# Hybrid decoder layer on one core: lo parts of weights by accumulating transfers, a fused softmax mask and maximum, decays built by transfers

## The chip, the cores and the metric

The kernel runs on one core of a Trainium2 chip. The core has five instruction streams that run beside each other: TensorE (PE, matrix products; its loads of the stationary operand are shown as PEld), VectorE (DVE), ScalarE (ACT), GpSimd (POOL) and SyncE (SP), which only issues transfers here. Sixteen DMA engines carry the transfers of all streams. Products are accumulated in PSUM; everything else lies in SBUF. Each stream takes its instructions strictly in order.

The metric is the device time of one execution, in microseconds (us). Three runs of the kernel before gave 473.19, 473.93 and 474.29 us; the median is 473.93.

## The reference

One decoder layer of 512 tokens and 1024 channels, in float32. The input is normalised, projected by one matrix of 1024 x 4384, and feeds three head groups. Their outputs are gated, concatenated (1536 wide), projected back, added to the input and normalised.

```
proj = rmsnorm(x) @ w_in
A: kc, vc = compress(k_c), compress(v_c)        # blocks of 32 tokens every 16, 2048 -> 256 -> 64
   o_a = g0*attend(q, kc, vc) + g1*attend(q, k_s, v_s, selected) + g2*attend(q, k_w, v_w, window)
B: a_cs = cumsum(dt * a) per chunk of 128 tokens
   decay_in = exp(where(causal, a_cs[l] - a_cs[s], -inf))
   y = ((C @ B.T) * decay_in) @ xdt + (C @ state) * exp(a_cs) + x * d_skip   # scan over 4 chunks
C: o_c = softmax(q @ km.T / sqrt(128)) @ vm,  km, vm = rmsnorm(mem) @ w_mem_kv
out = rmsnorm(x + [silu(gate)*o_a, norm(y*silu(z)), silu(gate)*o_c] @ w_out)
_masked_softmax: s = where(mask, s, -1e30); p = exp(s - max(s)) * mask; p / max(sum(p), 1e-30)
```

With 512 tokens all blocks are selected and the window reaches back to the start, so the selected and the window branch are both plain causal attention, over their own keys and values: 8 heads, 2 branches, 2 groups of keys.

## The kernel before

**Exactness by two parts.** Products run in float32r, PE's fast form of float32 with a shorter mantissa. Every operand that needs full precision is therefore split: hi is the operand rounded to float32r, lo the rest, and a product is taken as hi x hi, lo x hi and hi x lo, accumulated in one PSUM tile. Weights are split too. `chunk` (L379-390) does that for one block of at most 128 x 1024: SP loads it into `wst` (2 slots), ACT or DVE copies it into `whi`, and DVE or POOL subtracts `wst - whi` into `wlo` (3 slots each). There are 64 such blocks: 28 column tiles of the input projection (`wd`), the two halves of z (`wz0`, `wz1`), the values (`wv`), the compression (`w1k`, `w1v`), memory keys and values (`wmk`, `wmv`) and the output projection in three shares (`wob`, `wox`, `woa`). The first of all is forced onto ACT.

**What sets the order.** The program is recorded as streams, and a list scheduler (`Program.issue`, L173) puts the instructions of each engine in an order that is fixed when the kernel is built. It uses its own costs (`Program.cost`, L137), by which a transfer takes 60 ns of its issuing engine and 2000 ns plus bytes/360 until it lands, on one shared transfer resource. Of the instructions that could go it takes the first of the program, shifted by a bias; some instructions may go to either of two engines, and the one that is free takes them (`AnyEngine`, L290: a copy to ACT or DVE, a two-operand operation to DVE or POOL). On the chip every engine then follows its list, and waits where an operand is late.

**Stages.** First the input rows are normalised and turned, and the z projection starts. Then come the eight convolution tiles of group B with z's other half, then, woven together, the scan of group B (`ssd_decay`, `ssd_mix`, `ssd_out`) and the compressed keys and values, memory keys and values, rotated keys and value rows. From about 211 us on attention (`attention`, L733) is woven with the query and gate tiles, group C (`xa_scores`, `xa_apply`) and the output shares of groups B and C (`out_part`, L1078). The output projection of group A ends the run (`out_proj`). `out_part` takes two blocks for each half of the columns and uses both until the half is through.

**Softmax of A.** For each pair of heads `t` and each query block `i` (0 to 3), `soft` (L662) takes units of (head, branch) pairs: four in one tile for `i` = 0, two for `i` = 1, one from `i` = 2 on. Scores over `(i+1) * 128` keys stand in PSUM. DVE adds the causal mask to the last 128 columns, DVE takes the negated maximum, ACT takes the exponential with that as bias and sums it (an extra read-out instruction of ACT follows each). `soft_div` (L680) clamps the sums, takes their reciprocal and scales the probabilities by reciprocal and gate; for single-pair units this is one instruction with two scalars on DVE or POOL, L696:

```
X.scale(p[:, 0], p[:, 0], den[:, 2, c:c + 1], gate[...])
```

`apply` then turns the probabilities on PE (`pt`), splits them into `pth` and `ptl` and multiplies by the values.

**Decays of B.** `ssd_dt` writes the 32 rows of running sums to DRAM (`a_rows`). `ssd_decay` (L1000) makes, for each chunk `c`, a tile R of 128 x (8 heads x 128): SP loads the rows broadcast over the partitions, DVE subtracts the running sum of each partition, POOL adds the causal mask, ACT takes the exponential in one instruction. PE uses R in `ssd_mix` after a product with C and B.

Of the kernel before, what the change touches and what calls it, by code (L numbers as in the profile page):

```python
# [14 lines left out]
OP = mybir.AluOpType  # L15
# [14 lines left out]
C_ID, C_TRI, C_CAUS, C_MT, C_CADD, C_CMUL, C_II, C_INV, C_SGN, C_END = (  # L30
    0, 128, 256, 384, 512, 640, 768, 830, 831, 832)
# [3 lines left out]
# slots of the tags in SBUF and PSUM  # L35
B4, T2, M8, QB, PB, XB_, WS, WH = 2, 5, 12, 5, 4, 2, 2, 3
SB, TB, JB = 2, 2, 3
# shares at which streams are interleaved, and how far their instructions are put before (-) or
# behind (+) their place in the program when more than one could go
# [9 lines left out]
def shape_constants():  # L49
# [3 lines left out]
    c[:, C_CAUS:C_CAUS + P] = np.where(k <= r, 0.0, NEG)  # L53
    c[:, C_TRI:C_TRI + P] = r <= k
    c[:, C_MT:C_MT + P] = np.where(k >= r, 0.0, NEG)
# [19 lines left out]
class Program:  # L75
    """The instructions of a kernel, recorded in program order and issued in the order of a list
    scheduler: each engine takes, of the instructions whose operands and tiles are there, the
    first of the program. A tile takes a slot of its tag only if the tiles of the program before
    it still find theirs."""
# [32 lines left out]
    def record(self, *ways):  # L112
        """One instruction, with each engine that may run it: (engine, function, args, kw)."""
# [23 lines left out]
    def cost(self, eng, fn, outs, ins, kw):  # L137
# [4 lines left out]
        if fn == "dma_start":  # L142
            b = 4 * n * outs[0].shape[0]
            return 60.0, 2000.0 + b / 360.0
# [145 lines left out]
class AnyEngine:  # L290
    """Instructions that more than one engine can run."""
# [33 lines left out]
def hymba_kernel(ctx: ExitStack, tc: tile.TileContext, A, out):  # L325
# [11 lines left out]
    def f(ap):  # L337
        return ap.bitcast(F32)
# [28 lines left out]
    caus = cst[:, C_CAUS:C_CAUS + P]  # L367

# [10 lines left out]
    def chunk(src, n, st=None, first=False):  # L379
        if st is None:  # L380
            st = wp.tile([P, WMAX], F32, name="wst", tag="wst", bufs=WS)[:, :n]
        SY.dma_start(st, src)
        hi = wp.tile([P, WMAX], F32R, name="whi", tag="whi", bufs=WH)[:, :n]
        lo = wp.tile([P, WMAX], F32R, name="wlo", tag="wlo", bufs=WH)[:, :n]
        if first:
            SC.activation(hi, st, AF.Copy)
        else:
            X.copy(hi, st)
        X.tensor_tensor(lo, st, f(hi), op=OP.subtract)
        return hi, lo  # L390

# [82 lines left out]
    # compressed keys and values: blocks of 32 tokens, every 16  # L474
# [83 lines left out]
    # keys of the selected and the window branch  # L558
# [15 lines left out]
    # values of both branches and the gates: token rows  # L574
# [87 lines left out]
    def soft(t, i, unit, den, ps2):  # L662
        """Scores of a unit of (head, branch) pairs and their exponentials, with the sums."""
# [7 lines left out]
        V.tensor_tensor(s[:, :, i * P:n * P], s[:, :, i * P:n * P], caus.unsqueeze(1).to_broadcast([P, u, P]), op=OP.add)  # L671
        nm = kp.tile([P, u], F32, name="nm", tag="nm", bufs=8)
        V.tensor_reduce(nm, s, axis=AX.X, op=OP.max, negate=True)
        p = kp.tile([P, u, n * P], F32, name="pr", tag="pr", bufs=PB)
        for x, (e, b) in enumerate(unit):
            c = 2 * e + b
            SC.activation(p[:, x], s[:, x], AF.Exp, bias=nm[:, x:x + 1], accum_out=den[:, 0, c:c + 1])
# [3 lines left out]
    def soft_div(t, i, units, den, ps):  # L681
        """Exponentials by their sums, times the gates."""
# [4 lines left out]
        V.tensor_scalar(den[:, 1, c0:c1], den[:, 0, c0:c1], 1e-30, None, op0=OP.max)  # L687
        V.reciprocal(den[:, 2, c0:c1], den[:, 1, c0:c1])
# [3 lines left out]
        for unit, p in zip(units, ps):  # L692
            e, b = unit[0]
            c, u = 2 * e + b, len(unit)
            if u == 1:
                X.scale(p[:, 0], p[:, 0], den[:, 2, c:c + 1], gate[:, i, 6 * t + 3 * e + 1 + b:6 * t + 3 * e + 2 + b])  # L696
# [3 lines left out]
    def apply(t, i, ps2, pcs):  # L700
# [19 lines left out]
        if i % 2:  # L720
            # both parts together, times the gate path
# [152 lines left out]
    SD = {}  # L874

    def ssd_dt():
# [29 lines left out]
        V.tensor_copy(acs.rearrange("p a b -> p (a b)"), ps[:, 0])  # L906
        V.tensor_copy(lastb.rearrange("p a b -> p (a b)"), ps[:, 1])
# [15 lines left out]
        SD.update(dt=dt, acs=acs, arow=arow, eal=eal, dtd=dtd, dec=dec)  # L923
# [38 lines left out]
    def z_half(hf):  # L962
# [6 lines left out]
        for c in range(3 - hf):  # L969
            n = min(kc_, KT - kc_ * c) * w_  # L970
            st = kp.tile([P, WMAX], F32, name="wst0", tag="m8", bufs=M8)[:, :n] if hf == 0 and c == 2 else None
            ch.append(chunk(A[f"wz{hf}"][c][:, :n], n, st, hf == c == 0))
# [27 lines left out]
    def ssd_decay(c):  # L1000
# [9 lines left out]
        SY.dma_start(R, bass.AP(tensor=ar.tensor, offset=ar.offset + c * 8 * P, ap=[[0, P], [P, 8], [1, P]]))  # L1010
        V.tensor_tensor(R, R, SD["acs"][:, c].unsqueeze(2).to_broadcast([P, 8, P]), op=OP.subtract)
        G.tensor_tensor(R, R, cst[:, C_MT:C_MT + P].unsqueeze(1).to_broadcast([P, 8, P]), op=OP.add)
        SC.activation(R, R, AF.Exp)
# [62 lines left out]
    acc = []  # L1076

    def out_part(part):  # L1078
        """The share of head group B or C, onto the residual."""
# [73 lines left out]
    def weave(a, b, ca, cb):  # L1153
        """Both streams, each at its share of the tensor engine's time."""
# [164 lines left out]
```

## Time and profile before

| | |
|---|---|
| runs, median of three | 473.93 us |
| profiled execution, span from first to last instruction | 473.4 us |
| PE busy | 418.8 us (88%) |
| DVE busy | 405.6 us (86%) |
| POOL busy | 209.8 us (44%) |
| ACT busy | 180.5 us (38%) |
| mean granted clock of PE | 0.975 |
| SP's transfers | 44.54 MB, 28.6% of the 16 engines' time |

Of the profiled execution the span is what the trace shows; the runs' times also hold what lies around it. "Busy" counts an engine's instructions without their waits. PE's products overlap, and their ends are modelled, so a busy PE isn't a PE at its peak. All recorded instructions carry the same line (L278), since one line issues them; groups are told apart by the tiles they write and read.

### The profile page before, as it was taken

How to read it: one execution, taken by the hardware profiler on the slowest of the kernel's cores; microseconds unless marked ns; L12 is line 12 of the kernel's file. 1: busy time of each engine (PE TensorE's matmuls, PEld its weight loads, DVE VectorE, ACT ScalarE, POOL GpSimd, SP SyncE). 2: the span in 40 equal slices, each digit the busy share in tenths (PEclk: the TensorE clock that was granted, in tenths of full speed). 3: DMA queues.
4: the chain of work that ended last, by engine and by line, in shares of the span. 5: the costliest groups of instructions: out<-in, count | busy, mean ns of one | idle time of the engine just before them, and what ended most of it. 6: DMA issues, size and time to landing. Idle time of an engine off the chain costs nothing.

```text
span 473.4 us, 6323 instructions
## 1 busy us (share of the span) xinstructions
PE 418.8 (88%) x2291; PEld 350.0 (74%) x2291; DVE 405.6 (86%) x701; ACT 180.5 (38%) x402; POOL 209.8 (44%) x137
## 2 busy tenths in 40 slices
PE   3798969898796999998998997989989999799993
PEld 3786869678785888896877775868678776687872
DVE  4897886998999998898789999897998999968555
ACT  5333232544224023444444344434444435322324
POOL 3671322367576675624443224233434626402332
PEclk9898979999999899999999999899999999999998
DMA  8714520333553444213120120132113202203104
GB/s 321 266 53 131 174 66 4 111 112 94 174 160 108 134 134 141 90 45 132 48 90 0 46 79 11 46 134 90 44 46 126 97 0 91 61 29 90 44 1 177
DMA packets 15407, 44.95 MB, mean 95 GB/s; under 512 B 1648, under 2 KB 3984, under 8 KB 15376
## 3 DMA queue, kind: packets, MB, share of 16 engines
q1 hardware_dynamic: 15232, 44.54, 28.6%
q8 instruction: 18, 0.29, 0.3%
q14 instruction: 13, 0.11, 0.1%
q10 hardware_dynamic: 144, 0.01, 0.0%
HBM read 42.43 MB, written 2.11 MB: 94 GB/s over the span
## 4 chain that ended last, share of the span: by engine, by line
PE 42%; DVE 40%; issue 5%; ACT 3%; POOL 2%; DMA 1%; POOLq 0%; DVEq 0%; ACTq 0%
PE pj L278 13%; PE po L278 9%; PE pop L278 5%; DVE wlo L278 5%; DVE whi L278 5%; PE pt L278 3%; DVE den L278 3%; DVE pr L278 3%; PE pjz L278 3%; PE sc L278 2%; PE pjv L278 2%; DVE cacc L278 2%; DVE nm L278 2%; DVE ptl L278 2%; DVE o L278 2%
## 5 line engine op out<-in xcount | busy, mean ns | idle before, releaser
L278 POOL TENSOR_TENSOR wlo<-wst,whi 128x1024 fp32r<-128x1024 f32 (+2 forms) x34 | 82.2, 2419 | 97.7 <-DVE whi L278 33.9
L278 PE MATMUL pj<-xh,whi 128*128 128x512 f32 x224 | 91.4, 408 | 0.0
L278 PE MATMUL pj<-xh,wlo 128*128 128x512 f32 x224 | 90.5, 404 | 0.4 <-DVE wlo L278 0.3
L278 PE MATMUL pj<-xl,whi 128*128 128x512 f32 x224 | 89.9, 401 | 0.0
L278 PEld LDWEIGHTS pj<-xh,wlo 128*128 128x128 f32 x224 | 42.7, 190 | 8.8 <-DVE wlo L278 0.9
L278 PEld LDWEIGHTS pj<-xl,whi 128*128 128x128 f32 x224 | 42.7, 191 | 8.6 <-issue 0.3
L278 PEld LDWEIGHTS pj<-xh,whi 128*128 128x128 f32 x224 | 42.7, 190 | 7.9 <-DVE gxt L278 0.4
L278 DVE TENSOR_TENSOR wlo<-wst,whi 128x1024 fp32r<-128x1024 f32 (+2 forms) x30 | 45.7, 1522 | 1.8 <-PE pjz L278 0.7
L278 ACT ACTIVATE pr<-sc,nm 128x128 f32<-128x128 f32 (+3 forms) x64 | 33.2, 525 | 36.1 <-DVE nm L278 16.5
L278 ACT ACTIVATE whi<-wst 128x1024 fp32r<-128x1024 f32 (+3 forms) x31 | 31.7, 1023 | 25.4 <-DMA wst<-in_wd 5.9
L278 PE MATMUL pt<-cst,pr 128*128 128x128 f32 x160 | 31.4, 279 | 8.7 <-DVE pr L278 6.9
L278 DVE CAST whi<-wst 128x1024 fp32r<-128x1024 f32 (+1 forms) x33 | 32.2, 977 | 6.6 <-PE pj L278 3.4
L278 PEld LDWEIGHTS pt<-cst,pr 128*128 128x128 f32 x160 | 19.4, 140 | 16.4 <-DVE pr L278 9.1
L278 PE MATMUL sc<-kst,qst 128*128 128x512 f32 (+2 forms) x96 | 29.5, 368 | 1.1 <-ACT pr L278 1.1
L278 DVE TENSOR_TENSOR ptl<-pt,pth 128x512 fp32r<-128x512 f32 x40 | 27.1, 682 | 1.4 <-ACT pth L278 1.0
L278 DVE TENSOR_REDUCE nm<-sc 128x1 f32<-128x384 f32 (+3 forms) x44 | 27.7, 633 | 0.3
L278 POOL TENSOR_SCALAR pr<-pr,den,gate 128x512 f32<-128x512 f32 (+1 forms) x11 | 9.0, 821 | 40.6 <-DVE den L278 24.9
L278 PE MATMUL pop<-whi,oph 128*128 128x512 f32 x64 | 26.4, 415 | 0.1
L278 ACT ACTIVATE pth<-pt 128x512 fp32r<-128x512 f32 x23 | 13.7, 596 | 33.2 <-PE pt L278 33.1
L278 PE MATMUL pop<-whi,opl 128*128 128x512 f32 x64 | 25.6, 403 | 0.0
L278 PE MATMUL pop<-wlo,oph 128*128 128x512 f32 x64 | 25.5, 401 | 0.0
L278 PE MATMUL po<-ptl,vst 128*128 128x256 f32 x80 | 22.0, 293 | 1.7 <-DVE ptl L278 1.7
(287 smaller groups left out, 1076.1 us busy)
## 6 DMA issues: line engine op xcount, KB each, us to landing
wst<-in_wd SPq DMA_DIRECT2D x28, 512.0 KB, 3.3
x<-in_x SPq DMA_DIRECT2D x8, 512.0 KB, 4.2
R<-a_rows SPq DMA_DIRECT2D x4, 512.0 KB, 4.3
wst<-in_w1k SPq DMA_DIRECT2D x4, 512.0 KB, 3.5
wst<-in_wmk SPq DMA_DIRECT2D x4, 512.0 KB, 3.6
wst<-in_w1v SPq DMA_DIRECT2D x4, 512.0 KB, 3.5
wst<-in_wmv SPq DMA_DIRECT2D x4, 512.0 KB, 3.6
wst<-in_wob SPq DMA_DIRECT2D x4, 512.0 KB, 3.6
```

Of the source, the lines that this page charges most:

```text
L278: o["ins"] = getattr(self.engines[o["eng"]].engine, o["fn"])(*o["args"], **o["kw"])
```

## The change

1. Every weight block but the first three (`wz0`) gets its lo part another way. ACT writes `-wst` rounded to float32r into `wlo`; `whi` is a copy as before (ACT or DVE); and a transfer issued by POOL adds the block, read a second time from DRAM, onto `wlo`. The three blocks of `wz0` keep the subtraction.
2. The scheduler's cost of a transfer from POOL is 1000 ns of POOL and 2000 ns plus bytes/180 until it lands.
3. Mask and maximum of the softmax are one DVE instruction per (head, branch) pair over all `(i+1) * 128` columns: it writes minus (scores plus mask), and the minimum of that. The mask lies in one constant of 512 columns, three blocks of zeros ahead of the triangle, of which the last `(i+1) * 128` are used. The exponential has a scale of -1. The table of constants grows from 832 to 1088 columns.
4. The clamp of the sums goes. Single-pair units are scaled on ACT: one instruction of one column for reciprocal times gate, one for the probabilities.
5. R is first loaded with the mask (eight copies of a new 128 x 128 input), then the rows are added by a transfer from POOL, and the negated running sum is the bias of eight exponentials, one per head.

```diff
         if fn == "dma_start":
             b = 4 * n * outs[0].shape[0]
+            if eng == "POOL":
+                return 1000.0, 2000.0 + b / 180.0
             return 60.0, 2000.0 + b / 360.0
...
-    def chunk(src, n, st=None, first=False):
+    def chunk(src, n, st=None, first=None):
...
-        if first:
-            SC.activation(hi, st, AF.Copy)
-        else:
-            X.copy(hi, st)
-        X.tensor_tensor(lo, st, f(hi), op=OP.subtract)
+        if first is not None:
+            if first:
+                SC.activation(hi, st, AF.Copy)
+            else:
+                X.copy(hi, st)
+            X.tensor_tensor(lo, st, f(hi), op=OP.subtract)
+            return hi, lo
+        SC.activation(lo, st, AF.Copy, scale=-1.0)
+        X.copy(hi, st)
+        G.dma_start(lo, src, accum_op=OP.add)
         return hi, lo
...
-        V.tensor_tensor(s[:, :, i * P:n * P], s[:, :, i * P:n * P], caus.unsqueeze(1).to_broadcast([P, u, P]), op=OP.add)
         nm = kp.tile([P, u], F32, name="nm", tag="nm", bufs=8)
-        V.tensor_reduce(nm, s, axis=AX.X, op=OP.max, negate=True)
+        mask = cst[:, C_CAUS + (3 - i) * P:C_CAUS + 4 * P]
+        for x in range(u):
+            V.tensor_tensor_reduce(out=s[:, x], in0=s[:, x], in1=mask, scale=-1.0, scalar=3e38, op0=OP.add, op1=OP.min,
+                                   accum_out=nm[:, x:x + 1])
...
-            SC.activation(p[:, x], s[:, x], AF.Exp, bias=nm[:, x:x + 1], accum_out=den[:, 0, c:c + 1])
+            SC.activation(p[:, x], s[:, x], AF.Exp, bias=nm[:, x:x + 1], scale=-1.0, accum_out=den[:, 0, c:c + 1])
...
-        V.tensor_scalar(den[:, 1, c0:c1], den[:, 0, c0:c1], 1e-30, None, op0=OP.max)
-        V.reciprocal(den[:, 2, c0:c1], den[:, 1, c0:c1])
+        V.reciprocal(den[:, 2, c0:c1], den[:, 0, c0:c1])
...
-                X.scale(p[:, 0], p[:, 0], den[:, 2, c:c + 1], gate[:, i, 6 * t + 3 * e + 1 + b:6 * t + 3 * e + 2 + b])
+                g0 = 6 * t + 3 * e + 1 + b
+                SC.activation(den[:, 3, c:c + 1], den[:, 2, c:c + 1], AF.Copy, scale=gate[:, i, g0:g0 + 1])
+                SC.activation(p[:, 0], p[:, 0], AF.Copy, scale=den[:, 3, c:c + 1])
...
-            ch.append(chunk(A[f"wz{hf}"][c][:, :n], n, st, hf == c == 0))
+            ch.append(chunk(A[f"wz{hf}"][c][:, :n], n, st, c == 0 if hf == 0 else None))
...
-        SY.dma_start(R, bass.AP(tensor=ar.tensor, offset=ar.offset + c * 8 * P, ap=[[0, P], [P, 8], [1, P]]))
-        V.tensor_tensor(R, R, SD["acs"][:, c].unsqueeze(2).to_broadcast([P, 8, P]), op=OP.subtract)
-        G.tensor_tensor(R, R, cst[:, C_MT:C_MT + P].unsqueeze(1).to_broadcast([P, 8, P]), op=OP.add)
-        SC.activation(R, R, AF.Exp)
+        SY.dma_start(R, A["mt"].unsqueeze(1).to_broadcast([P, 8, P]))
+        G.dma_start(R, bass.AP(tensor=ar.tensor, offset=ar.offset + c * 8 * P, ap=[[0, P], [P, 8], [1, P]]),
+                    accum_op=OP.add)
+        for h in range(8):
+            SC.activation(R[:, h], R[:, h], AF.Exp, bias=SD["nacs"][:, c, h:h + 1])
```

`nacs`, the negated running sums, is one small DVE instruction in `ssd_dt`.

## Rows read from the trace of the kernel before

**Rows 1.** Stages: start:end, length, busy us of each engine, PE clock, transfer share, GB/s.
```profile
0.00:30.00 30.00, 19.16 (x120) 18.02 (x121) 22.10 (x41) 13.35 (x25) 18.63 (x18) 0.94 0.65 232
30.00:105.00 75.00, 66.22 (x335) 56.30 (x334) 61.97 (x88) 28.13 (x45) 27.02 (x14) 0.93 0.33 102
105.00:180.00 75.00, 64.29 (x443) 58.53 (x443) 70.29 (x88) 20.97 (x40) 50.82 (x32) 0.98 0.42 132
...
211.00:443.00 232.00, 216.60 (x1120) 172.37 (x1119) 207.54 (x411) 95.01 (x241) 87.60 (x56) 0.99 0.20 66
...
sum 474.00, PE 418.75 PEld 349.95 DVE 405.61 ACT 180.54 POOL 209.80; mean PE 69.79 PEld 58.33 DVE 67.60 ACT 30.09 POOL 34.97
```

**Rows 2.** The chain that ended last, shares of the span by engine.
```profile
PE 42%; DVE 40%; issue 5%; ACT 3%; POOL 2%; DMA 1%; POOLq 0%; DVEq 0%; ACTq 0%
```

**Rows 3.** Waits of PE: us in total, times, longest us.
```profile
PE pt L278 <- DVE pr L278: 6.9, 9, 2.4
PE pjm L278 <- DVE wlo L278: 4.5, 3, 1.8
PE pxs L278 <- DVE xst L278: 4.0, 1, 4.0
```

**Rows 4.** The page's groups of the split: busy us, mean ns, idle before.
```profile
L278 POOL TENSOR_TENSOR wlo<-wst,whi 128x1024 fp32r<-128x1024 f32 (+2 forms) x34 | 82.2, 2419 | 97.7 <-DVE whi L278 33.9
...
L278 DVE TENSOR_TENSOR wlo<-wst,whi 128x1024 fp32r<-128x1024 f32 (+2 forms) x30 | 45.7, 1522 | 1.8 <-PE pjz L278 0.7
...
L278 ACT ACTIVATE whi<-wst 128x1024 fp32r<-128x1024 f32 (+3 forms) x31 | 31.7, 1023 | 25.4 <-DMA wst<-in_wd 5.9
```

**Rows 5.** Instructions of the tile whi: duration in ns, minimum/median/maximum.
```profile
L278 DVE CAST whi<-wst x33: 423/694/2506, 14.8 to 448.6; 128x1024 fp32r<-128x1024 f32 x32, 128x528 fp32r<-128x528 f32 x1
```

**Rows 6.** Stages, instructions of wlo alone: PE, PEld, DVE, POOL.
```profile
30.00:105.00 75.00, 33.30 (x106) 18.83 (x106) 7.32 (x6) 15.65 (x6) 0.93 0.33 102
105.00:180.00 75.00, 34.98 (x114) 22.33 (x114) 22.50 (x14) 8.14 (x4) 0.98 0.42 132
...
211.00:443.00 232.00, 74.05 (x183) 34.63 (x182) 4.59 (x4) 48.60 (x20) 0.99 0.20 66
```

**Rows 7.** Groups kept apart by shape: POOL's smallest operation, busy us, mean ns.
```profile
L278 POOL TENSOR_TENSOR rx<-rx,mhalf 128x1 f32<-128x1 f32 x6 | 4.7, 781 | 7.3 <-DVE rx L278 6.5 <-DVE cwh L278 0.8
```

**Rows 8.** Transfers: the queue's share of 16 engines; issues, KB each, us to landing.
```profile
q1 hardware_dynamic: 15232, 44.54, 28.6%
...
wst<-in_wd SPq DMA_DIRECT2D x28, 512.0 KB, 3.3
...
mf<-in_memt SPq DMA_DIRECT2D x2, 512.0 KB, 8.5
```

**Rows 9.** The chain in order of time: start, us, work.
```profile
442.99 22.44 PE po L278 x96
```

**Rows 10.** Instructions of the tile sc, minimum/median/maximum ns.
```profile
L278 ACT ACTIVATION_READ_ACCUMULATOR pr<-sc,nm x64: 188/198/220, 209.1 to 427.5; 128x1 f32 x64
L278 DVE TENSOR_TENSOR sc<-sc,cst x44: 272/292/699, 207.4 to 424.2; 128x128 f32<-128x128 f32 x32, 128x256 f32<-128x256 f32 x8, 128x512 f32<-128x512 f32 x4
```

**Rows 11.** The page's group of the maxima.
```profile
L278 DVE TENSOR_REDUCE nm<-sc 128x1 f32<-128x384 f32 (+3 forms) x44 | 27.7, 633 | 0.3
```

**Rows 12.** Groups kept apart by shape: clamp, exponentials, subtraction in R.
```profile
L278 DVE TENSOR_SCALAR den<-den 128x2 f32<-128x2 f32 x24 | 11.5, 478 | 0.9 <-ACT pr L278 0.8
...
L278 ACT ACTIVATE pr<-sc,nm 128x512 f32<-128x512 f32 x16 | 10.8, 685 | 13.8 <-PE pt L278 9.5 <-DVE st L278 2.8 <-DVE nm L278 1.5
...
L278 DVE TENSOR_TENSOR R<-R,acs 128x1024 f32<-128x1024 f32 x4 | 8.3, 2082 | 0.0
...
L278 ACT ACTIVATE pr<-sc,nm 128x128 f32<-128x128 f32 x16 | 5.7, 366 | 6.8 <-PE pt L278 6.8
```

**Rows 13.** Instructions of the tile den, minimum/median/maximum ns.
```profile
L278 DVE TENSOR_SCALAR den<-den x28: 154/160/2166, 213.6 to 429.3; 128x2 f32<-128x2 f32 x24, 128x4 f32<-128x4 f32 x4
...
L278 DVE TENSOR_SCALAR pr<-pr,den,gate x21: 465/548/2502, 228.0 to 430.7; 128x384 f32<-128x384 f32 x11, 128x512 f32<-128x512 f32 x10
```

More of the change, by code (lines that the diff above doesn't have):

```diff
@@ L29 @@
        0.0014142135623842478, 0.00027424818836152554, 5.3182957344688475e-05, 1.0313385246263351e-05)
-C_ID, C_TRI, C_CAUS, C_MT, C_CADD, C_CMUL, C_II, C_INV, C_SGN, C_END = (
-    0, 128, 256, 384, 512, 640, 768, 830, 831, 832)
+C_ID, C_TRI, C_CAUS, C_CADD, C_CMUL, C_II, C_INV, C_SGN, C_END = (
+    0, 128, 256, 768, 896, 1024, 1086, 1087, 1088)
 P_GI, P_GM, P_CW, P_CB, P_DTB, P_AL, P_DS, P_PK, P_PV, P_W2K, P_W2V, P_GS, P_END = (
@@ L52, in shape_constants @@
     c[:, C_ID:C_ID + P] = r == k
-    c[:, C_CAUS:C_CAUS + P] = np.where(k <= r, 0.0, NEG)
+    c[:, C_CAUS + 3 * P:C_CAUS + 4 * P] = np.where(k <= r, 0.0, NEG)
     c[:, C_TRI:C_TRI + P] = r <= k
-    c[:, C_MT:C_MT + P] = np.where(k >= r, 0.0, NEG)
     for i in range(NT):
@@ L366, in hymba_kernel @@
     ident = cst[:, C_ID:C_ID + P]
-    caus = cst[:, C_CAUS:C_CAUS + P]
     def biased(b, gen):
@@ L906, in ssd_dt @@
         V.tensor_copy(acs.rearrange("p a b -> p (a b)"), ps[:, 0])
+        nacs = cp.tile([P, NT, 8], F32, name="nacs")
+        V.tensor_scalar(nacs.rearrange("p a b -> p (a b)"), ps[:, 0], -1.0, None, op0=OP.mult)
         V.tensor_copy(lastb.rearrange("p a b -> p (a b)"), ps[:, 1])
@@ L922, in ssd_dt @@
         SC.activation(dec, lastb, AF.Exp)
-        SD.update(dt=dt, acs=acs, arow=arow, eal=eal, dtd=dtd, dec=dec)
+        SD.update(dt=dt, nacs=nacs, arow=arow, eal=eal, dtd=dtd, dec=dec)
     def ssd_xbc(t):
@@ L1300, in layout @@
     r["cst"] = shape_constants()
+    r["mt"] = np.where(np.arange(P)[None, :] >= np.arange(P)[:, None], 0.0, NEG).astype(f32)
     return {k: np.ascontiguousarray(v) for k, v in r.items()}
```

## Prediction

> **What bounds the kernel now.** I read five views in this order: the table of stages, the chain that ended last, the waits of TensorE (PE), the groups of instructions, the transfers.
>
> In the table of stages [rows 1] the reader is to see two engines near their limit at once. PE is busy 418.75 us and VectorE (DVE) 405.61 us of a 473.4 us span. PE's idle time is a stage's length less its busy time there: 10.8 us in 0-30 (start), 8.8 in 30-105 (convolution inputs), 10.7 in 105-180 (compressed keys, memory keys and values, scan), 15.4 in 211-443 (attention, with the output shares of B and C). DVE is at 94% in 105-180 and 89% in 211-443. The chain gives PE 42% and DVE 40% of the span [rows 2]: the two hand work to each other. What PE waits for in these stages is mostly DVE [rows 3]: scaled probabilities, lo parts of weights, a convolved tile. So relieving DVE can pay, up to the 34.9 us that PE idles in the last three of these stages, if nothing else arrives later than DVE does now.
>
> **Weights.** 64 blocks are split into hi and lo; the first three of the run stay as they are, so 61 change.
> - Gone: the subtraction, 1.52 us on average on DVE (30 of them, 45.7 us) and 2.42 on GpSimd (POOL; 34, 82.2 us) [rows 4]. Less the three that stay (one, and two), DVE loses 44 us and POOL 77.
> - Added on ScalarE (ACT): one negated copy per block, as long as the hi copy there, 1.02 us [rows 4]: 61 x 1.02 = 62 us. ACT then gives hi copies away: up to 28 go to DVE, where the median is 0.69 [rows 5], so DVE gets back up to 19 us.
> - Added on POOL: the issue of one transfer. The trace has none issued there. Below it is nothing, above it the subtraction replaced, 2.42; I take 1.0, nearest to POOL's smallest operation, 0.78 [rows 7]. 61 x 1.0 = 61 us. The issue waits for ACT's copy, and POOL is in order: the scan's products, the rotary sums and the power operations stand behind it. POOL falls from 209.8 to about 180 us all the same.
> - Added in the queues: 61 accumulating transfers, of which the trace has none. A plain 512 KB load lands in 3.3 us, the slowest of that size in 8.5 [rows 8]. SP's queue is 28.6% of 473.4 us = 135.4 us for 44.54 MB, so 512 KB occupy the 16 engines for 1.6 us. An accumulation is at least such a passage (1.6) and, reading two operands, at most about two (3.2). I take 2.4, the middle: reading doubles, writing doesn't. Then it lands in 3.3 + 0.8 = 4.1 us, and a lo part is ready 1.0 + 1.0 + 4.1 = 6.1 us after its block has come; today it is copy plus subtraction, 0.7 + 1.5 to 1.0 + 2.4.
>
> Where this lies beside other work and where not:
> - 30-105: a column tile of 24 products takes 24 x 0.23 = 5.6 us of PE (96 products in 22.44 us, [rows 9]); three lo slots give 16.8 us per cycle, against 6.1 + 5.6. Hidden.
> - 105-180: 18 blocks [rows 6] and 3 decay tiles in 75 us, each with little PE work (a memory-key block has 24 products of 256 columns, a compression block 8). Transfers are busy 0.42 x 75 = 31.5 us now. After: 21 x (1.6 + 2.4) = 84 us, 9 more than the stage is long; at the lower end 21 x 3.2 = 67, nothing. Against it, the 14 subtractions that DVE has here, 22.5 us [rows 6], go, and with them PE's 4.5 us of waits on lo parts and some of its waits behind DVE's queue. I take +9 less 6 = **+3 us**, ends -7 and +19.
> - The output shares hold two blocks for a whole half, with three slots; so the second block of the next half can begin only when the half before is through, and its first product is due 6 x 0.23 = 1.4 us into the half. There are four such changes and that to the final projection. Attention's work covers the early ones. An uncovered one costs the later arrival, 6.1 less about 3 = 3 us; I count one, **+3 us** (ends 0 and +12).
>
> A rule that speaks against the change: the Trainium skill, "Collectives: The Full Stack", section "The bandwidth ceiling: the fold count and why AG ≠ RS ≠ AR", says that an adding transfer issues two source reads on the same ring and runs at about half the rate of a copy (32.35 against 62.28 GB/s in its table); no accumulation is in this trace. By it the 2.4 is 3.2, and the first rival below is the outcome.
>
> **Softmax.** It runs 16 times for each number of key blocks, 1 to 4, so there are 64 (head, branch) maxima.
> - Now: 44 mask additions, 32 x 0.29 + 8 x 0.42 + 4 x 0.70 = 15.4 us (median and maximum in [rows 10], 0.42 between them), and 44 reductions, 27.7 us [rows 11].
> - After: 64 fused passes with PSUM in and out. At the addition's 0.29 for 128 columns and 0.70 for 512, 16 x (0.29 + 0.42 + 0.56 + 0.70) = 31.5 us. Whether the second output costs a read-out isn't shown: at least 0, at most ACT's 0.20 [rows 10], 0 to 12.8 us. I take half, 6.4. Sum 38 against 43: -5 us of DVE (ends -12 and +1; a pass at half speed, +26).
> - The clamp: 28 instructions, of which the 24 on two columns took 11.5 us, 0.48 on average [rows 12]; but the median is 0.16, and some stood up to 2.17 us [rows 13], while POOL was at work. Gone: -12 us of DVE, and from the path between the sums and PE's transposes. The reciprocal then follows the sums directly.
> - Scaling: 21 multiplications on DVE (median 0.55, worst 2.50; some 15 us) [rows 13] and the 11 on POOL become 32 on ACT, 16 x 0.69 + 16 x 0.58 = 20 us by the exponentials of 512 and 128 columns [rows 12], and 32 one-column products, between the read-out's 0.20 and 0.37, I take 0.28: 9 us. That adds some 0.4 us to a path from sum to transpose, and takes away the clamp and the stays beside POOL. On ACT the hi halves of turned probabilities queue behind; ACT has room, 95 of 232 us now.
>
> In 211-443 DVE goes from 207.5 to about 207.5 - 4.6 (four subtractions, [rows 6]) - 12 - 15 - 5 + 9 (hi copies from ACT) = 180 us, 78%; ACT to some 95 + 29 + 24 (24 negated copies) - 9 = 139 us, 60%. Of PE's 15.4 us of idle time there, 6.9 wait on scaled probabilities alone [rows 3]; with DVE at 78% instead of 89% I let two thirds of it go, and 2 us of products that now stand isolated close up: **-12 us** (ends -3 and -20).
>
> **Decays.** Four tiles lose 2.08 us each on DVE [rows 12] and as large an addition on POOL; they get a mask load (in place of the rows' load), an accumulation of rows issued by POOL, and eight exponentials of 128 columns, at up to 0.37 each, instead of one large one. 4.1 + 1.0 + 3.0 from rows to decay replaces load, two passes and an exponential, about as long. DVE -8 us in all, half of it in 30-105. There PE waits 4.0 us for a convolved tile on DVE [rows 3], and DVE also loses six subtractions, 7.3 us [rows 6]: I take half of the 8.8 us of idle time, **-4 us** (ends 0 and -7).
>
> **The sum.** 473.4 + 3 + 3 - 12 - 4 = 463.4 us of span. The start and the last products are as they were, but for a constant load 128 KB longer beside the first loads, hidden. The median of the runs shown, 473.93, is 0.5 above the span, so **464 us**. Late next: PE itself in attention, the transfers in 105-180. The forecast's own range is 455 to 472.
>
> **Rivals.**
> 1. *The transfers become the bound* (slower). At 3.2 us for an accumulation, 105-180 needs 21 x 4.8 = 101 us, +26 less the 6; with -12 - 4 and +6 for the changes of halves, 473.9 + 10 = **484**. It decides from about 2.7 us on, where 21 x 4.3 = 90, +15 - 6 + 6 - 16 = -1. For it: that stage uses each block so shortly. Against it: transfers are busy only 0.20 of the attention stage, and three slots let some blocks come early.
> 2. *PE gets most of its idle time back.* At 1.6 us an accumulation is a load like any other; 105-180 falls by 7, 30-105 by 5, attention by 15, and the changes of halves are covered: 473.9 - 27 = **447**. For it: DVE's long instructions are rare stays (0.16 against 2.17, 0.55 against 2.50, 0.69 against 2.51), which end with POOL's long passes. Against it: part of PE's idle time follows the order of the list.
> 3. *Hidden anyway.* The chain from scores to transposes moves to ACT and is as long as before; attention gives 3, 30-105 gives 2, the transfers take 5: **474**. For it: PE is 93% busy in attention.
>
> **How the numbers follow.** Forecast 0.42, rival 1 0.30, rival 2 0.18, rival 3 0.10. About 0.2% (1 us) is what can be told from no change. Faster: 0.42 + 0.18 + 0.02 of rival 3 = 0.62; same 0.06; slower 0.30 + 0.02 = 0.32. The range 447 to 487 takes in both outer rivals' times and rival 1 with an uncovered change more; beyond it stand a fused pass at half speed and accumulations as slow as the 8.5 us load.
>
> **What would show it.** After: three subtractions on POOL and DVE together, DVE near 340 us, PE near 419, ACT near 270. Right: 211-443 shorter by some 12 us, with little waiting for scaled probabilities. Wrong: PE waiting for transfers into lo parts, a transfer share near 1.0 where the memory keys are made, or accumulations that land later than 5.5 us (rival 1); a fused pass over 0.9 us at 512 columns.

## The result and the profile after

Four runs of the changed kernel gave 507.74 to 517.3 us, median **511.82**, against 474.11 for the kernel before beside them: a ratio of 1.0755 [1.0694, 1.0815]. The change makes the kernel 7.5% slower; 464 was forecast, with 487 as the upper end. The profiled execution has a span of 515.5 us; its run, 517.3, is the longest of the four, so its stages are some 5 us long beside the median; the ratios leave out executions that are slowed at a lower granted clock, as this one is, and the medians count them.

The first view is the page of after: the busy line, the queues, the chain's shares, then groups and issues.

```profile
PE 433.7 (84%) x2291; PEld 363.8 (71%) x2291; DVE 331.4 (64%) x713; ACT 238.1 (46%) x511; POOL 145.8 (28%) x146
...
q0 software_dynamic: 9360, 33.66, 36.5%
q1 hardware_dynamic: 18816, 44.67, 27.6%
...
PE 45%; DMA 25%; issue 12%; DVE 11%; POOL 3%; ACT 3%; POOLq 0%; SPq 0%; ACTq 0%
...
L279 ACT ACTIVATE wlo<-wst 128x1024 fp32r<-128x1024 f32 (+2 forms) x61 | 63.5, 1045 | 95.5 <-PE pj L279 45.6
L279 DVE CAST whi<-wst 128x1024 fp32r<-128x1024 f32 (+1 forms) x48 | 34.9, 727 | 44.6 <-PE pj L279 31.9
L279 POOL DMA_DIRECT2D wlo<-in_wd x28 | 25.1, 896 | 114.1 <-ACT wlo L279 103.4
...
wst<-in_wd SPq DMA_DIRECT2D x28, 512.0 KB, 5.2
wlo<-in_wd POOLq DMA_DIRECT2D x28, 512.0 KB, 7.7
...
R<-a_rows POOLq DMA_DIRECT2D x4, 512.0 KB, 11.0
wst<-in_w1k SPq DMA_DIRECT2D x4, 512.0 KB, 8.5
```

DVE fell by 74 us, to 331, and the time rose all the same. In the chain that ended last DVE went from 40% to 11%, and DMA from 1% to 25% [rows 2]: a quarter of that chain is now transfers, and a ninth of it DVE's work. The last lines show what became late: a lo part lands 7.7 us after its issue, and the plain loads of the same tiles land in 5.2 where they took 3.3 [rows 8].

The next view is the table of stages with the four windows of [rows 1], same columns, and under them two windows cut at after's own borders: 107 (the last convolved tile is turned), 249 (the last value product), 482 (the final projection begins).

```profile
0.00:30.00 30.00, 17.60 (x119) 16.27 (x120) 23.06 (x42) 13.42 (x24) 16.47 (x17) 1.00 0.78 271
30.00:105.00 75.00, 58.56 (x301) 49.49 (x300) 39.25 (x81) 35.38 (x62) 17.79 (x18) 0.89 0.74 164
105.00:180.00 75.00, 56.35 (x319) 49.52 (x319) 40.75 (x67) 26.81 (x50) 32.36 (x33) 0.88 0.90 204
211.00:443.00 232.00, 216.09 (x1139) 178.25 (x1140) 174.89 (x417) 124.67 (x301) 51.75 (x52) 0.97 0.54 125
...
107.00:249.00 142.00, 114.97 (x646) 102.34 (x645) 73.69 (x141) 50.84 (x90) 55.34 (x55) 0.86 0.81 181
249.00:482.00 233.00, 217.44 (x1125) 176.08 (x1124) 176.61 (x419) 126.30 (x313) 46.29 (x48) 0.98 0.52 120
```

And the kernel before at the same borders of its own work:

```profile
100.00:210.00 110.00, 98.35 (x642) 88.91 (x642) 101.14 (x136) 36.88 (x73) 71.05 (x45) 0.98 0.37 116
210.00:443.00 233.00, 217.60 (x1126) 173.27 (x1125) 208.54 (x413) 95.81 (x245) 87.60 (x56) 0.99 0.20 66
```

Equal times are not equal work here, so the last two rows of each are the ones to compare: the count of products (646 and 642, 1125 and 1126) says that they hold nearly the same work. Keys and values take 142 us instead of 110. Attention takes 233 us in both, though DVE went from 208.5 to 176.6 us in it. In 105 to 180 the share of the transfers rose from 0.42 [rows 1] to 0.90. They don't fill the whole of keys and values, though: 0.81 of 142 us are 115 us, and windows of 10 us inside that stage go from 0.48 to full (last column but one):

```profile
137.00:147.00 10.00, 7.21 (x38) 6.56 (x38) 4.47 (x6) 3.90 (x10) 5.24 (x5) 0.66 1.07 256
177.00:187.00 10.00, 7.25 (x39) 7.28 (x40) 4.06 (x8) 3.50 (x5) 5.44 (x5) 0.66 0.48 103
```

PE's waits (us in total, times, longest) now name transfers in most of the places where [rows 3] named DVE, and hi copies beside them; the scaled probabilities are down to 0.8:

```profile
PE pj L279 <- DMA wlo<-in_wd: 17.3, 3, 9.4
...
PE pjm L279 <- DVE whi L279: 3.8, 2, 2.8
PE pj L279 <- DVE whi L279: 3.7, 1, 3.7
PE pjm L279 <- DMA wlo<-in_wmk: 3.3, 2, 2.0
...
PE pjm L279 <- DMA wlo<-in_wmv: 3.0, 2, 1.9
...
PE ph L279 <- DMA wlo<-in_w1k: 2.5, 1, 2.5
...
PE pt L279 <- ACT pr L279: 0.8, 1, 0.8
```

All accumulations of weights together, from the view of the tile `wlo`:

```profile
DMA to landing us min/median/max: 5.1/7.9/11.9
```

### The profile page after: what moved, and what is told of

It reads as the page before. It is cut to its first block, busy times and chain, and to the rows that moved or that the text cites. A ratio compares the mean times of both kernels' runs of the same rounds, so it can differ in the third digit from the quotient of the medians.

```text
span 515.5 us, 6502 instructions
## 1 busy us (share of the span) xinstructions
PE 433.7 (84%) x2291; PEld 363.8 (71%) x2291; DVE 331.4 (64%) x713; ACT 238.1 (46%) x511; POOL 145.8 (28%) x146
## 3 DMA queue, kind: packets, MB, share of 16 engines
q0 software_dynamic: 9360, 33.66, 36.5%
## 4 chain that ended last, share of the span: by engine, by line
PE 45%; DMA 25%; issue 12%; DVE 11%; POOL 3%; ACT 3%; POOLq 0%; SPq 0%; ACTq 0%
PE pj L279 23%; DMA wlo<-in_wd 5%; PE po L279 5%; PE pop L279 3%; PE pjm L279 3%; DMA wst<-in_w1k 2%; PE pt L279 2%; PE sc L279 2%; DMA R<-a_rows 2%; DMA wlo<-in_w1k 2%; DMA wlo<-in_wmv 2%; DMA wst<-in_wd 2%; DMA wlo<-in_wmk 2%; DMA wst<-in_wmv 2%; DMA wlo<-in_w1v 1%
## 5 line engine op out<-in xcount | busy, mean ns | idle before, releaser
L279 ACT ACTIVATE wlo<-wst 128x1024 fp32r<-128x1024 f32 (+2 forms) x61 | 63.5, 1045 | 95.5 <-PE pj L279 45.6
L279 PE MATMUL pj<-xh,wlo 128*128 128x512 f32 x224 | 92.7, 414 | 17.3 <-DMA wlo<-in_wd 17.3
L279 PE MATMUL pj<-xh,whi 128*128 128x512 f32 x224 | 93.4, 418 | 4.3 <-DVE whi L279 3.7
L279 DVE CAST whi<-wst 128x1024 fp32r<-128x1024 f32 (+1 forms) x48 | 34.9, 727 | 44.6 <-PE pj L279 31.9
L279 POOL DMA_DIRECT2D wlo<-in_wd x28 | 25.1, 896 | 114.1 <-ACT wlo L279 103.4
L279 PE MATMUL pt<-cst,pr 128*128 128x128 f32 x160 | 33.1, 277 | 1.0 <-ACT pr L279 0.8
L279 DVE CUSTOM_DVE_ANT_0 sc<-sc,cst 128x128 f32<-128x128 f32 (+3 forms) x64 | 31.1, 494 | 2.0 <-PE sc L279 1.5
L279 DVE CAST pth<-pt 128x512 fp32r<-128x512 f32 x21 | 14.5, 690 | 17.0 <-PE pt L279 16.9
L279 PEld LDWEIGHTS pt<-cst,pr 128*128 128x128 f32 x160 | 20.5, 140 | 5.4 <-ACT pr L279 1.3
L279 DVE SCALAR_TENSOR_TENSOR cacc<-pj,cwh,cacc 128x509 f32<-128x509 f32 (+2 forms) x24 | 17.9, 747 | 8.7 <-ACT cacc L279 8.3
L279 PE MATMUL po<-pth,vst 128*128 128x256 f32 x80 | 22.4, 285 | 0.0
```

Of the source, the lines that this page charges most:

```text
L279: o["ins"] = getattr(self.engines[o["eng"]].engine, o["fn"])(*o["args"], **o["kw"])
```

## The experiments

Each is compared with the kernel before on the same chip, and the ratio to it, with its interval, is given behind the median in us. Differences between two experiments are differences of medians, unless a ratio is named. "Parts" are those of the change's list.

**Parts 1 and 2 alone.**

> The kernel before with the change's lo parts of weights alone (61 accumulating transfers, the planner's cost of them), softmax and decays as before. Theory T (the transfers are the loss): the stage of compressed and memory keys grows as in the changed kernel, from about 57 to 85 us, and the whole takes 500 to 515 us. Rival S (the softmax or the decays on ScalarE lose it): at most 485 us.

510.89, 1.0724 [1.0652, 1.0797]: inside theory T's range. The weights alone bring the whole loss, and the other parts change nothing that can be told on top of them: 511.82 with all.

**Part 5 alone** (with its cost line).

> The kernel before with the change's decays alone: mask load, accumulated rows, eight exponentials. Theory T: a small effect, 470 to 478 us, since only four accumulations run beside an otherwise half idle queue. Rival S: over 480 us. The prediction's own step said 4 us less, 470.

463.40, 0.9749 [0.9693, 0.9805]: a gain of 12 us (2.5%), more than any of the three forecasts. Its convolution stage ends at 91 us instead of 100; the row of that stage, and PE's waits on DVE that lie in it:

```profile
30.00:91.00 61.00, 58.61 (x315) 49.79 (x315) 48.04 (x81) 30.36 (x56) 17.55 (x10) 0.97 0.40 117
```

```profile
PE pcs__148 L280 <- DVE dw L280: 2.1, 1, 2.1
...
PE pj L280 <- DVE wlo L280: 0.3, 1, 0.3
```

PE idles 2.4 us there (61 - 58.61), against 8.8 in 30 to 105 before, and the wait for a convolved tile, 4.0 us in [rows 3], is gone.

**Parts 3, 4 and 5, weights as before.**

> The changed kernel with the weights' lo parts subtracted as before: softmax and decays as changed. The prediction's steps say 12 + 4 us less than before, 458 us. Theory T allows that, 456 to 468 us. Rival H (attention isn't held up by VectorE, so relieving it there pays nothing): 470 to 478 us. Rival S: over 480 us.

463.04, 0.9714 [0.9655, 0.9772]. The softmax adds nothing that can be told to the decays' gain; 458, by the prediction's steps, was not reached. This full computation is the fastest one here, with part 5 alone beside it. Its stages, cut as above, are what the weights are measured against:

```profile
92.00:200.00 108.00, 100.63 (x642) 90.89 (x641) 91.48 (x139) 41.38 (x88) 65.58 (x46) 0.95 0.43 128
200.00:432.00 232.00, 216.88 (x1124) 173.06 (x1124) 193.15 (x415) 113.15 (x295) 71.75 (x41) 0.99 0.20 66
```

By the ends of the stages, after loses against this kernel 15.4 us up to the last convolved tile (106.9 and 91.5), 33.8 in keys and values (which end at 249.3 and 200.1), 1.0 in attention and 2.6 behind it. A loss per block would be spread over the run; this one falls where blocks come close together.

**Is it the planner's wrong idea of the landing?** The order is laid out again for transfers that land 4.4 us behind their 2.9 us on the queue, 7.3 in all, near the measured 7.9.

```diff
-                        end = dma + 2000.0
+                        end = dma + (4400.0 if e == "POOL" else 2000.0)
```

> The changed kernel with one number of the planner changed: a transfer from GpSimd is reckoned to land 4.4 us after its turn on the queue instead of 2.0, so 7.3 us after issue for 512 KB on an idle queue, near the 7.9 us measured. All instructions and bytes are the same, only the order differs. Theory T1 (16 engines' time is what lacks in the keys' stage): 500 us or more, that stage stays above 80 us. Theory T2 (the lists were laid out for transfers that land at 4.9 us, so engines stand behind waits in the wrong places): 485 us or less.

512.28, 1.0766 [1.0709, 1.0822]. No: theory T1's side.

**Is it the bytes, or the adding?** Same order, same bytes, plain copies; the lo parts are then not lo parts.

```diff
-        G.dma_start(lo, src, accum_op=OP.add)
+        G.dma_start(lo, src)
```

> The changed kernel with the 61 weight transfers from GpSimd as plain copies (the block is written over the lo tile instead of being added to it, so the lo parts are not the rest of the split; everything else, the planner's costs included, is the same, and so is the order). A plain copy should hold the 16 engines 1.6 us instead of 2.95. Theory T1 (time of the 16 engines): most of the 49 us between the changed kernel and the one without weight transfers comes back, 470 to 482 us. Theory T3 (the way over GpSimd, issue and landing, whatever the bytes do): less than half comes back, 490 us or more.

483.26, 1.0146 [1.0077, 1.0215]: 28.5 us come back, more than half, though T1's upper end was 482. The queue's line, that of the kernel without weight transfers, where only the four additions of rows into R are on it, and the landing:

```profile
q0 software_dynamic: 9360, 33.66, 22.8%
```

```profile
q0 software_dynamic: 576, 2.10, 2.4%
```

```profile
DMA to landing us min/median/max: 3.5/4.8/8.6
```

In after the queue holds the 16 engines for 36.5% of 515.5 = 188.2 us; 33.66 MB are 64.2 blocks of 512 KB, so 2.93 us each. Here it is 22.8% of 475.9 = 108.5 us, of which the rows of R, that still add, take 2.4% of 462.7 = 11.1; the 60.2 blocks of weights take 97.4, so 1.62 us each, no more than a plain load (1.6). Adding costs 1.8 times a copy, on the same queue, for the same blocks. The rule of the Trainium skill weighed in the prediction ("Collectives: The Full Stack", "The bandwidth ceiling: the fold count and why AG ≠ RS ≠ AR"), half the rate for an adding transfer, asks for 1.93 by its table, which compares two collectives; the 1.8 here comes near it. The hold isn't all that shrinks with the adding: the landing goes from 7.9 to 4.8 us, and the issue on POOL from 866 to 541 ns (median of the 28 of `in_wd`). So this run shows that the adding costs 28.5 us, and not by which of the three.

**An eighth of the bytes, still adding, same order.** 16 of 128 partitions are transferred; the planner's cost stays that of the whole block, so that the order stays too.

```diff
-                return 1000.0, 2000.0 + b / 180.0
+                return 1000.0, 2000.0 + b * (8 if outs[0].shape[0] == 16 else 1) / 180.0
...
-        G.dma_start(lo, src, accum_op=OP.add)
+        G.dma_start(lo[:16], src[:16], accum_op=OP.add)
```

> The changed kernel (511.8 us) in the same order of every engine, but each of the 61 weight transfers adds only the first 16 of 128 partitions (an eighth of the bytes, on all 16 engines; the other lo parts lack the addition). Every wait stays. Theory T1 (time of the 16 engines): nearly all of the 49 us come back, at most 470 us. Theory T2 (fixed way: copy, issue, landing): 490 us or more. Half and half: about 480.

480.12, 1.0092 [1.0072, 1.0113]. Its stage of keys and values, and the landing:

```profile
95.00:220.00 125.00, 104.77 (x647) 93.22 (x646) 77.09 (x141) 50.74 (x90) 53.00 (x55) 0.93 0.46 123
```

```profile
DMA to landing us min/median/max: 2.8/4.1/6.1
```

31.7 us of the weights' 48.8 go with the bytes; 17.1 stay, the half and half of the forecast, with transfers busy 0.46 and landings of 4.1 us, the very landing that the prediction counted with. Plain copies of all the bytes leave 20.2, only 3 more, and their stage of keys and values is as long: 124.8 us, against 125.3 here (both by the ends of the stages). So it is the adding of the bytes, more than their number, that went. What stays looks different: in this window PE waits for hi copies on DVE and hardly for lo parts, and ACT's negated copies, which need a free lo slot, wait for PE's products:

```profile
PE pjm L279 <- DVE whi L279: 8.1, 3, 3.2
...
PE pjm L279 <- DMA wlo<-in_wmv: 1.0, 1, 1.0
```

```profile
ACT wlo L279 <- PE pj L279: 13.0, 5, 6.6
ACT wlo L279 <- PE ph L279: 8.6, 2, 6.7
```

**Late blocks only, and blocks of keys only.** The adding path is taken for the blocks named in `USE` and `WD`, else the subtraction stays.

```diff
-        if first is not None:
+        if first is not None or not (src.tensor.name in USE and (src.tensor.name != "in_wd" or src.offset // (P * D) in WD)):
```

> Softmax and decays as changed; accumulating lo parts only for the 27 blocks that attention and the output shares use (15 tiles of queries and gates, 12 of the output projection), the other 34 subtracted. The queue is busy for a fifth there. Theory T1: no loss, 458 to 466 us against 463 without weight transfers. Theory T3 (each late landing costs, above all where two blocks are held at once): 475 us or more.

465.46, 0.9733 [0.9641, 0.9824]: 27 of the 61 blocks, used in attention and behind it, cost 2.4 us over the kernel without them by the medians and 0.9 by the ratios (0.9733 and 0.9714), which can't be told from nothing. Theory T3 is out: their lo parts land in 7.4 us (median), almost as late as in after, and attention is as long as without them, 231.6 us. A late landing by itself costs nothing where blocks are far apart.

> Softmax and decays as changed; accumulating lo parts only for the 16 blocks of compression and memory keys and values, the other 45 subtracted. Theory T1: the larger part of the loss, 16 x 2.95 us on a queue that is near half busy there: 480 to 495 us. Theory T3: about 16 of 61 parts of it, 470 to 478 us.

491.54, 1.0353 [1.0275, 1.0430]: the 16 blocks of compressed and memory keys and values cost 28.5, as theory T1 had it.

**The same 16 with an eighth of the bytes.**

> The kernel with accumulating lo parts for the 16 blocks of compression and memory keys and values alone (491.5 us), same order, each transfer with an eighth of its bytes. Theory T1: back to 463 to 468 us. Theory T2: 482 us or more.

476.54, 1.0027 [1.0002, 1.0053]: between the two forecasts. 15.0 of the 28.5 go with the bytes, 13.5 stay.

**A fourth lo slot for them,** paid for with two slots of another tag (`T2`, 5 to 3), and a control with only that taken.

```diff
-B4, T2, M8, ... = 2, 5, 12, ...
+B4, T2, M8, ... = 2, 3, 12, ...
-        lo = wp.tile([P, WMAX], F32R, name="wlo", tag="wlo", bufs=WH)[:, :n]
+        lo = wp.tile([P, WMAX], F32R, name="wlo", tag="wlo", bufs=4)[:, :n]
```

> As the kernel with accumulating lo parts for the 16 blocks of compression and memory keys and values alone (491.5 us), but with four slots for lo parts instead of three, paid for by the half-row work tile's slots going from five to three. Theory T1 (time of the 16 engines): nothing to gain, 488 to 496 us. Theory T2 (a landing of 8 us that three slots can't cover): 482 us or less. To be read against the next one.

489.63, 1.0320 [1.0284, 1.0357]. By itself this is theory T1's nothing to gain.

> Control for the four slots: softmax and decays as changed, weights as before (463.0 us), with the half-row work tile's slots going from five to three and nothing else. 463 to 470 us by either theory.

470.22, 0.9905 [0.9868, 0.9942]. The control lost 7 us by the slots taken from the other tag, and over it the slotted kernel loses 19.4 us instead of 28.5. That speaks for the slots as a part of what stays, but both kernels also have another order, and 9 us are hardly more than an order does alone (below).

**Why did attention not get shorter?** First, 27.2 us of PE's products are left out there: the third product of 15 query and gate tiles, 120 products.

```diff
+            ways = ((hi, xh), (lo, xh), (hi, xl)) if idx not in LESS else ((hi, xh), (lo, xh))
```

> Softmax and decays as changed, weights as before; the third product (rest of the input by hi weights) of the 15 query and gate tiles in attention is left out: 120 products, 0.227 us apart, 27.2 us of TensorE, whose operands have long been ready, so no wait of another engine goes with them. Rival H: 434 to 440 us. The prediction's step: 450 us or more.

443.52, 0.9347 [0.9310, 0.9384]: 19.5 us less than with them, between the two forecasts and nearer rival H's. Second, DVE's 64 fused passes are left out; the exponential takes the raw scores.

```diff
-            V.tensor_tensor_reduce(out=s[:, x], in0=s[:, x], in1=mask, ...)
...
-            SC.activation(p[:, x], s[:, x], AF.Exp, bias=nm[:, x:x + 1], scale=-1.0, accum_out=den[:, 0, c:c + 1])
+            SC.activation(p[:, x], s[:, x], AF.Exp, bias=AT["zero"], accum_out=den[:, 0, c:c + 1])
```

> Softmax and decays as changed, weights as before; the 64 fused passes of mask and maximum are left out (the exponential reads the bare scores, so the probabilities aren't the reference's). VectorE loses some 38 us in attention, and each unit's way from scores to exponentials a pass and two waits. Rival H (TensorE's own work and order set attention's length): 458 to 464 us against 463. The prediction's step (the chain over VectorE sets it): 452 us or less.

460.80, 0.9716 [0.9671, 0.9760]: 2.2 us less by the medians and nothing by the ratios (0.9716 and 0.9714), in rival H's range, though DVE has 20.5 us less to do in attention. (The passes and their read-outs took 40 us; other instructions that may go to either of two engines filled a part of that.) The two rows of that stage, first without the products, then without the passes:

```profile
197.00:410.00 213.00, 192.15 (x1009) 153.77 (x1009) 191.00 (x412) 113.23 (x302) 71.90 (x41) 0.98 0.20 62
```

```profile
197.00:428.00 231.00, 218.34 (x1128) 176.32 (x1128) 172.66 (x303) 106.90 (x285) 70.04 (x39) 0.98 0.21 67
```

The stage follows PE: 19 us shorter than the 232 of the kernel with everything in it, for 24.7 us less PE work, and 1 us shorter for DVE's 20.5. Each was run in one order only, so the 1 us by itself proves little; the 19 are more than twice what an order did (below). A third one left out the 80 products of `ptl` with the values:

> Softmax and decays as changed, weights as before, and TensorE's 80 products of the probabilities' lo parts with the values left out (the lo parts are still made, so the other engines do the same). They stand 0.117 us apart, 9.4 us in all. If TensorE's own work sets attention's length (rival H): 452 to 456 us. If the chain over VectorE and ScalarE sets it, as the prediction had it: 461 to 464 us.

446.42, 0.9411 [0.9364, 0.9459]: 16.6 us less, below both forecasts. It points the same way, but PE then no longer waits for `ptl` either, so by itself it decides nothing.

**How much is the order alone?** The planner's cost of a semaphore is raised; what changes is where an instruction stands in its engine's list, and for a few which of two engines takes it (DVE runs 703 instead of 701, POOL 135 instead of 137).

```diff
-    SEM = 60.0
+    SEM = 75.0
```

> The kernel before with one number of the planner changed that says nothing of the chip's work (a semaphore reckoned at 75 ns instead of 60), so the same instructions in another order. If the decays' gain of 12 us is their own, this moves by less: 470 to 478 us. If a new order alone can move that much, it may fall outside.

483.10, 1.0159 [1.0103, 1.0216]: the kernel before, 7.5 us slower by another order than beside it in the first, and outside the forecast. So the parts were measured once more in this second family.

> The decays' part alone, in the second family of orders (semaphore reckoned at 75 ns), against 483.1 us for the kernel before in that family. If the decays' gain is their own: 468 to 474 us. If it was a lucky order: 478 us or more.

472.84, 0.9936 [0.9903, 0.9970].

> Softmax and decays in the second family of orders. If attention is bound by TensorE, within 5 us of the decays alone there; if the softmax part has a gain of its own that the first order hid, 460 us or less.

467.89, 0.9836 [0.9776, 0.9895].

> The whole change in the second family of orders. If the transfers lose it, in whatever order: 505 to 525 us. If much of the 49 us was the order: 495 us or less.

516.95, 1.0758 [1.0675, 1.0841].

All three came out as the first of their two forecasts had it, the softmax at the edge (5.0 us). By the ratios, with 475 us for 1:

| part | first order | second order |
|---|---|---|
| decays | 0.9749 - 1, -11.9 us | 0.9936 - 1.0159, -10.6 us |
| softmax | 0.9714 - 0.9749, -1.7 us | 0.9836 - 0.9936, -4.8 us |
| weights | 1.0755 - 0.9714, +49.4 us | 1.0758 - 0.9836, +43.8 us |

Each ratio's interval reaches 0.003 to 0.008 to either side, 2 to 4 us. So decays and weights keep their size within the noise; the softmax lies somewhere between nothing and 5 us of gain. By the ends of the stages, the weights lose 16.3 us up to the last convolved tile in the second order, 26.2 in keys and values, 0.6 in attention and 4.0 behind it: the same two stages. The decays' gain has no fixed place: in the first order the last convolved tile is turned 8.9 us earlier and the rest gives 1.3 more, in the second it is 4.7 there and 6.7 in keys and values.

The parts don't add. Weights alone cost 34 us over the kernel before (ratio 1.0724), but 49 over the kernel with the other parts: what decays and softmax gain without the weights' transfers, 14 us, is gone with them.

## Why the prediction was wrong

**The step that failed is the weights' transfers**, hidden in 30 to 105, +3 in 105 to 180 and +3 at the changes of halves, where the runs show +34 by themselves and +44 to +49 on top of the other parts. Four things in it were off.

- *The size of an accumulation.* Taken 2.4 us of the 16 engines, measured 2.93. This is beyond the 2.7 from which rival 1 was to decide. That the adding is the larger part is shown by the plain copies: same bytes, same order, 28.5 us back. But the price alone doesn't make the loss: 2.93 in the prediction's own sum gives 21 x 4.53 = 95 us for 105 to 180, +20 less 6 = +14 instead of +3, and 475 us in all. The sum for this stage counted the time of the engines as its only bound, and in keys and values they were busy 115 of 142 us.
- *The landing.* Taken 4.1 us, measured 7.9 (median). The 4.1 was a plain load's 3.3 and 0.8 for the longer passage, as if the transfer had the engines for itself; but the plain loads beside it land later too (5.2 for 3.3), plain copies in its place land in 4.8, and the 27 late blocks alone still land in 7.4, so most of the delay is the addition's own. So a lo part is ready 1.05 + 0.90 + 7.9 = 9.9 us after its block, not 6.1. The rows added into R, taken at 4.1 too, land in 6.4 to 7.4 where the weights don't accumulate, in 11.0 here. Hold and landing rise together wherever blocks accumulate; which of them costs how much among the keys stays open.
- *Where it bites.* The prediction held 30 to 105 for hidden (16.8 us per cycle of three slots, against 6.1 + 5.6). With 9.9 + 5.6 it would still be hidden by that sum, yet 15.4 us were lost there. The sum counted blocks that come one after another, each with the transfers for itself; their share rose from 0.33 [rows 1] to 0.74. With an eighth of the bytes the last convolved tile is turned at 94.9 us, 3.4 behind the kernel without accumulation, with plain copies at 93.3: the adding is the larger part here as well. The changes of halves, feared instead, cost little: late blocks 1 to 2 us in all, within the noise.
- *The fixed way.* 17.1 us stay when seven eighths of the bytes are gone. In this are the negated copy, the issue that waits for it, a landing of 4.1 instead of a pass of 1.5, a lo slot held that much longer, and an order that was written for other costs. The fourth slot and the waits of ACT's negated copies on PE make the slot likely; how the 17 divide was not settled.

**Rival 1 came nearest, and was too small**: 484. It had +26 less 6 for its stage at a price of 3.2, more than was measured, and no loss ahead of it. Keys and values lost 34 us and the convolutions 15. Its mechanism, engines that are full, holds for a part of the stage only (1.07 and 0.48 in the windows above). Part of the 34 isn't waiting: PE's busy time there is 114.97 us for 646 products, against 100.63 for 642. The same memory-key products show it, in the view of the tile `pjm` (ns, minimum/median/maximum), first of after, then with the weights as before:

```profile
L279 PE MATMUL pjm<-mh,wlo x32: 278/400/582, 121.1 to 159.7; 128*128 128x256 f32 x32
```

```profile
L279 PE MATMUL pjm<-mh,wlo x32: 278/283/469, 102.5 to 124.4; 128*128 128x256 f32 x32
```

The granted clock of that stage is 0.86 instead of 0.95, so part of it was spent at 1.2 rather than 2.4 GHz, and PE waited 27 us in it instead of 7. That the waits brought the clock down was not tried by itself; with an eighth of the bytes, PE waits 20 us and the clock is 0.93, with plain copies 18 us and 0.92.

**Attention, -12, did not come.** The load came off DVE as worked out: 180 us forecast in that stage, 176.6 measured, and ACT 139 forecast, 126. The inference failed: that PE's idle time would go with DVE's load. The clean case is the kernel with weights as before, where no weight transfer comes in between: its waits on scaled probabilities fell from 6.9 us [rows 3] to 1.1, others took their place, and PE was busy 217 us of 232, as before.

```profile
PE po L279 <- DVE ptl L279: 3.8, 6, 1.3
...
PE pt L279 <- DVE pr L279: 1.1, 1, 1.1
```

In the changed kernel, 217 of 233 us, waits for accumulated lo parts take 6.5 us of the idle time. The stage follows PE's products more than DVE's work (17 to 20 us for 27.2 left out, 0 to 2 for DVE's 20.5, each in one order). Rival 3 had the argument, "PE is 93% busy in attention", but not the way: it expected a chain as long as before, now over ACT, and the waits at its end went.

**Decays, -4, brought some -11** where the weights don't accumulate. The step took half of PE's 8.8 idle us as the gain; in part 5 alone the last convolved tile is turned 8.9 us earlier (90.8, before 99.7), with 2.4 us of idle time left, and the final projection begins 10.2 us earlier, so nothing of it is given back. Of the 4, some was for subtractions that this kernel still has, so the term was low by more than the difference. Why the gain is as large in the second order, but half of it elsewhere, was not settled. In the changed kernel it doesn't show at all.

**Sizes that held.** Issue on POOL 0.90 us (1.0 taken), negated copy 1.045 (1.02), and from the groups kept apart by shape:

```profile
L279 DVE CUSTOM_DVE_ANT_0 sc<-sc,cst 128x512 f32<-128x512 f32 x16 | 10.9, 694 | 0.1
...
L279 DVE DVE_READ_ACCUMULATOR2_ANT nm<- 128x1 f32 x64 | 8.8, 138 | 0.1
...
L279 ACT ACTIVATE R<-R,nacs 128x128 f32<-128x128 f32 x32 | 10.1, 390 | 4.7 <-DMA R<-a_rows 4.7
...
L279 ACT ACTIVATE pr<-pr,den 128x512 f32<-128x512 f32 x16 | 10.6, 707 | 0.0
...
L279 ACT ACTIVATE den<-den,gate 128x1 f32<-128x1 f32 x32 | 7.6, 286 | 5.2 <-DVE den L279 5.2
```

The fused pass was taken at 0.70 and its read-out at 0.10 (0.138 here), the scaling at 0.69 and 0.28; only the exponential of R, at most 0.37 and measured 0.39, came out above its bound. DVE ended at 331 us (340 forecast); ACT at 238 (270), POOL at 146 (180). The loads of these three came out as worked out or lighter, and the time was wrong by 48 us: it hung on the weights' transfers, whose price and landing no row showed.

## What to carry to other kernels

Taking a pass off a busy engine with a second transfer is a trade of engine time against transfer time, and is judged in the stage where blocks follow one another fastest, not by the mean share (here 0.20 in attention, where 27 blocks cost 1 to 2 us, but 0.42 among the keys, where 16 cost 28). Where the price of the new transfer isn't in the trace and the forecast changes sign within its bounds, the bounds are the forecast; and its landing is to be counted beside the other transfers, not alone (4.1 us forecast here, 7.9 measured). Before an engine's relief is counted as a gain, see whether the other engine on the chain is itself busy nine tenths of the stage; and in a kernel whose order is planned, measure a part of 10 us in a second order before believing it.

## What the runs showed of the hardware

- An accumulation of 512 KB from DRAM into SBUF, issued by POOL, holds the 16 engines for 2.93 us, a plain copy on the same queue for 1.62; they land in 7.9 and 4.8 us (medians) in the same order of instructions.
- Issuing one of these transfers takes POOL 866 ns with the addition and 541 as a plain copy (medians of the 28 of `in_wd`).
- Transfers beside them land later: plain loads of `in_wd` went from 3.3 to 5.2 us (median; 4.3 beside plain copies of the same bytes), those of `in_w1k` from 3.5 to 8.5 (4.5). The four accumulations of rows broadcast from DRAM into R took 6.4 to 7.4 by themselves and 11.0 among the others.
- The minimum that DVE takes along with the fused pass is read out by an instruction of its own, 138 ns each, 64 times.
- A new order of the same instructions moved the kernel before by 1.6% [1.0, 2.2].
